# The attention gate as seven-product groups, and weight sums by DMA, in a two-layer hybrid block on one Trainium2 core

## The chip, the cores and the metric

The kernel runs on one core of one Trainium2 chip. The metric is the device time of one execution in microseconds, as the median of several runs. Beside the timed runs there is one profiled execution, from which all rows of the trace come.

## What is computed

Two layers of a block on 512 tokens and 16 meta tokens, 1024 wide, in float32. Cut to what matters here:

```
h = rms_norm(x, norm_g)
q, k, v, gate_a, u_b, gate_b, q_idx, k_idx, w_idx, merge = split(h @ w_in)
...
attn = indexer_sparse_attention(q, k, v, q_idx, k_idx, w_idx, k_top)   # top 128 keys a query
y_a = (attn * silu(gate_a)) @ w_a          # gate_a is 512 columns of w_in
y_b = (multiscale_pool(u_b) * silu(gate_b)) @ w_b
g_a, g_b = split(sigmoid(merge))           # merge is 2048 columns of w_in
return x + (g_a * y_a + g_b * y_b) @ w_out
```

## The kernel before

Every weight matrix is cut into chunks of 1 MB (256 columns of `w_in`), which are loaded, prepared and used in the order of the list `chunks`. A product in float32 is made of three matmuls of a faster type: the weights and the activations are each split into a high part (a rounded copy) and a low part (the rest), and high x high, high x low and low x high are summed in PSUM. `hhi` and `hlo` are the two parts of the normalised input.

A chunk is prepared in one of three ways. By `high`, `second` and `low` ScalarE casts and VectorE subtracts. For chunks in `by_dma`, ScalarE writes the negative low part's start, GpSimd adds the raw weights by an accumulating DMA (`minus`, L200 to L203), and ScalarE makes the high part (`plus`). The chunks in `mixed` are those of the merge gates: `mixed_prep` makes seven combinations of the chunk's four blocks a11, a12, a21, a22 (Winograd's form of a 2 x 2 block product), each as a high and a low part, in nine items `i0` to `i8`; its four sums of blocks are VectorE instructions (`mix`). The raw weights live in a ring of four half chunks (tag `raw`), so that a chunk's load waits for the chunk two ahead of it to be done with.

TensorE's order is written out by hand and so is VectorE's; ScalarE, GpSimd and the DMA queue of SyncE are ordered by a scheduler. A dense chunk (`dense`) takes 8 x 3 matmuls for each 128 output columns and each part of the tokens: two parts of 272 and 256 tokens in layer 0, one of 512 in layer 1. In `mix_gates` a chunk is a group of seven products of 12 matmuls each, 264 (layer 0) or 256 (layer 1) columns wide, whose operands are sums of the normalised input's quarters (`sums_of_h`, some by way of HBM in `far` and `hsheet`). After each product `end()` calls `group_done`, which runs what `later` has put off to this count, lets one preparation item run (and more until the list is `LEAD` ahead), and advances attention by `rate / 2` steps. `NEEDS` says which item a product waits for.

Attention is a generator (`attention`, three steps for each of 16 units u, made of two heads of one tile of 128 queries) that is woven between products by `fill` and `pump`. Its input is the top-k selection, 16 rounds of MAX8 and MATCH_REPLACE8 on VectorE, woven in by `sel` wherever the metered cost of VectorE (`dve_cost`, `FULL`) falls behind that of TensorE; `ensure` runs what is missing of it before a tile's logits. The gated result is written over `sa`, which holds the gate.

The order of a layer's stages is: keys and values with the indexer's queries; the pooled branch's gate (`sb`); the pooled branch's input; `queries(0)`; the attention gate (`sa`, two dense chunks, L1199 to L1209); `queries(1)`; the products with `w_b`, with attention woven in from here (L1224); eight seven-product groups for the merge gates; `w_a`; `w_out`.

Of the kernel before, what the change touches and what calls it, by code (L numbers as in the profile page):

```python
# [29 lines left out]
PB = 4  # L30
R_ATT = (1.95, 1.7)
FULL = 1.0
CAP = 1.5
# [47 lines left out]
def dve_cost(name, out, a=None, *rest):  # L81
    if name == "memset":
        return 0.1
    n = max(cols(out), cols(a))
    return 0.15 + n * (0.00052 if name in ("tensor_copy", "tensor_scalar") else 0.00104)


@with_exitstack
def tile_block(ctx: ExitStack, tc: tile.TileContext, x, meta, w_in, pool_w, w_a, w_b, w_out, rows, hgain, c_tab, out):
# [23 lines left out]
    mixed, by_dma, plain = set(), set(), set()  # L113
    metas = {7: 0, 10: 1}
    for l in range(2):
        wi = w_rows(w_in[l], 0, w_in.shape[2])

        chunks.append([(wi[:, :, 2176:2432], 0)])
        plain.add(len(chunks))
        chunks.append([(wi[:, :, 512:640], 0), (wi[:, :, 2688:2816], 128)])  # L120
        mb = [3784, 4040, 4296, 4552]
        order = [2432, 1664, 1920, 1408, 1152, 0, 640, 896, 256]
        chunks += [[(wi[:, :, c:c + 256], 0)] for c in order]
        chunks += [[(w_rows(w_b[l], c, 512), 0)] for c in (0, 512)]
        by_dma |= set(range(len(chunks) - 10, len(chunks)))
        mixed |= set(range(len(chunks), len(chunks) + 8))
        chunks += [[(wi[:, :, c:c + 256], 0)] for c in (*mb, 2760, 3016, 3272, 3528)]
        chunks += [[(w_rows(w_a[l], c, 512), 0)] for c in (0, 512)]
        chunks += [[(w_rows(w_out[l], c, 256), 0)] for c in (0, 256, 512, 768)]
# [4 lines left out]
    def w_place():  # L134
        c = W["load"]
        W["load"] += 1
        kt = chunks[c][0][0].shape[1]
        raws[c] = [wpool.tile([128, kt // 2, 2048 // kt], F32, tag="raw", name="raw", bufs=4) for s in range(2)]
# [25 lines left out]
    def w_prep_enqueue(casts_first=False, after=None):  # L164
# [40 lines left out]
        def plus(s):  # L205
            t = split(0)
            act.copy(t, raws[c][s])  # L207
            if s == 1:
                del raws[c]
                w_load()  # L210

        def highs():
# [11 lines left out]
        else:  # L224
            prep_q.extend((lambda: high(0), second, lambda: low(1)))

    def mixed_prep(c):

        r0, r1 = raws[c]
        blk = {"a11": r0[:, :, 0:128], "a21": r0[:, :, 128:256], "a12": r1[:, :, 0:128], "a22": r1[:, :, 128:256]}  # L230
        src = {"a11": "a11", "a12": "a12", "a22": "a22", "s3": "a11", "s2": "s2", "s1": "a21", "s4": "a12"}
        ops = ready[c]

        def hi(n):
            t = w_tile().rearrange("p (s k e) -> p s k e", s=2, k=4)
            ops[n] = t
            act.copy(t[:, 0], blk[src[n]])  # L237

        def lo(n):
            dve.tensor_sub(ops[n][:, 1], blk[src[n]], f(ops[n][:, 0]))  # L240

        def mix(eng, to, x, y, op):
            eng.tensor_tensor(blk[to], blk[x], blk[y], op=op)
# [371 lines left out]
    def q_post(t, ps, normed, dst, g=0):  # L615
# [18 lines left out]
        if normed and t == 0:  # L634
            norms()
        gp.tensor_tensor(t1[:m, :256], t1[:m, :256], t2[:m, :256], op=OP.add)
        if normed:
# [77 lines left out]
    def attention(ensure):  # L715
# [91 lines left out]

        for u in range(-1, 17):
            if u + 1 < 16:
                logits(u + 1)  # L810
# [56 lines left out]
    def sums_of_h(l, s0, n2):  # L867
# [7 lines left out]
        def sums(g):  # L875
            k = slice(2 * g, 2 * g + 2)
            a0, a1, b0, b1 = nf[0][:, k, c0], nf[0][:, k, c1], nf[1][:, k, c0], nf[1][:, k, c1]
            dve.tensor_tensor(a0, a1, a0, op=OP.subtract)
            dve.tensor_tensor(a1, b1, a1, op=OP.subtract)
            dve.tensor_tensor(b1, b1, a0, op=OP.subtract)  # L880
            dma(far[:, 0, g], a0)
# [3 lines left out]
        def lows(g):  # L885
            k = slice(2 * g, 2 * g + 2)
            a1, b0, b1 = nf[0][:, k, c1], nf[1][:, k, c0], nf[1][:, k, c1]
            dve.tensor_tensor(b0, b0, b1, op=OP.subtract)
            dma(far[:, 1, g], b0)
# [49 lines left out]
    def mix_gates(zb, ta, s0, n2, operands, splits, alos):  # L939
        base = popped[0] - progress[W["use"]]  # L940
        for q in range(8):
            c = W["use"]
# [3 lines left out]
            bs = [bank("d") for _ in range(3)]  # L946
            U, S, X = (bs[r] for r in ROLES[q % 3])
            done = [0]
# [10 lines left out]
            def end():  # L959
                done[0] += 1  # L960
                group_done()
                while prep_q and (popped[0] < base + 9 * q + LEAD + done[0] * 9 // 7 or (q == 7 and done[0] > 4)):
                    prep_one()

            def gate(eh, t, src, in_sheet):
                j = 2 * q + eh
                cs = slice(s0 + t * n2, s0 + (t + 1) * n2)
                if q < 4:
                    th = src if in_sheet else sheet(n2, "th")[:, :n2]
                    act.activation(th, src, AF.Tanh, scale=0.5)  # L970
                    d = zb[:, j, cs]
                    later(lambda: dve.scalar_tensor_tensor(d, th, 1.0, d, op0=OP.add, op1=OP.mult), 2)
                else:
                    act.activation(ta[j - KT][:, cs], src, AF.Tanh, scale=0.5)

            def total(eh, t, ps, part):
                o = sheet(n2, "c")[:, :n2]
                dve.tensor_tensor(o, ps[:, :n2], part, op=OP.add)
# [84 lines left out]
    for l in range(2):  # L1063
# [131 lines left out]

        queries(0)
        sa = one.tile([128, 4, T], F32, tag="D", name="sila")
        SIL["a"] = sa
        for c in range(2):  # L1199
            w = chunk()  # L1200
            for mi in range(2):
                j = 2 * c + mi
                for hf, a, n, o in halves:
                    ps = dense(w, mi, a, n)
                    th = sheet(n, "th")
                    act.activation(th[:, :n], ps[:, :n], AF.Tanh, scale=0.5)
                    later(lambda th=th, ps=ps, j=j, a=a, n=n: dve.scalar_tensor_tensor(
                        sa[:, j, a:a + n], th[:, :n], 1.0, ps[:, :n], op0=OP.add, op1=OP.mult), 1)
                    group_done()  # L1209
        queries(1)  # L1210

# [11 lines left out]

        fill.append(attend())  # L1224
        rate[0] = R_ATT[l]
        for _ in range(2):
# [30 lines left out]

        mix_gates(zb, ta, s0, n2, operands, splits, alos)
        drain()
# [153 lines left out]
```

## Time and profile before

| | |
|---|---|
| median of 3 runs | 758.84 us (757.47 to 760.31) |
| profiled execution | 756.37 us |
| its span, first to last instruction | 754.6 us |
| instructions in the profile | 15640 |
| granted TensorE clock | 1.00 |

PE is TensorE's matmuls, PEld its weight loads, DVE VectorE, ACT ScalarE, POOL GpSimd, SP SyncE, which issues most DMAs. Most TensorE and VectorE instructions are recorded under line 61, that of a helper, so they are told apart by their tiles: `d<-hhi,w` is a matmul of a weight tile `w` with `hhi` into the PSUM tile `d`. `lt` are attention's logits, `sc` the indexer's scores, `pm` the weights of the meta tokens, `pt` the turned weights. A matmul's own duration includes its way through the array, so the pace of TensorE is read from the distance between starts. Idle time stands in brackets, with what ended it.

### The profile page before, as it was taken

Reading aid. Unit: us, or ns where it says so; the run is one execution under the profiler, and the core shown is the slowest. Engines: PE = TensorE matmul, PEld = TensorE weight load, DVE = VectorE, ACT = ScalarE, POOL = GpSimd, SP = SyncE. Lnnn points to the kernel's source line nnn. Section 1 sums busy time; section 2 is a strip of 40 time slices with the busy share of each in tenths; the row PEclk is TensorE's granted clock in tenths of the full one; section 3 lists DMA queues with packets and bytes.
Section 4 is the critical chain, followed back from the end, with each engine's and each line's share of the span. In section 5 each row is a group of like instructions: output and inputs, shape, how many; then the busy total and the mean of one; then the engine's idle time right before and its main releaser. Section 6 shows DMA issues by size and latency. Waiting matters only on the chain.

```text
span 754.6 us, 15640 instructions
## 1 busy us (share of the span) xinstructions
PE 739.7 (98%) x5914; PEld 707.6 (94%) x5914; DVE 563.7 (75%) x1416; ACT 471.8 (63%) x1049; POOL 213.8 (28%) x280
## 2 busy tenths in 40 slices
PE   8999999999989999999999999999999999999998
PEld 7999999999989999999999989988989899999998
DVE  6866987889798775894358668787998888678531
ACT  7679645558869795543245786555677788764320
POOL 3741075242012100063256401741501011005100
PEclk9999999999999999999999999999999999999999
DMA  7677757775122223543422787667812322146411
GB/s 263 226 167 173 166 127 179 158 200 139 31 82 57 57 57 96 184 143 127 128 87 83 171 190 186 157 151 203 208 38 61 98 67 56 57 135 204 140 43 43
DMA packets 73547, 96.94 MB, mean 128 GB/s; under 512 B 3664, under 2 KB 58736, under 8 KB 73472
## 3 DMA queue, kind: packets, MB, share of 16 engines
q1 hardware_dynamic: 67632, 74.89, 31.9%
q0 software_dynamic: 5760, 20.97, 14.8%
q8 instruction: 46, 0.75, 0.4%
q14 instruction: 29, 0.24, 0.1%
q10 hardware_dynamic: 80, 0.08, 0.0%
HBM read 66.41 MB, written 8.55 MB: 99 GB/s over the span
## 4 chain that ended last, share of the span: by engine, by line
PE 81%; DVE 9%; ACT 6%; issue 1%; POOL 1%; DMA 1%; SPq 0%; DVEq 0%; ACTq 0%
PE d L61 69%; PE a L61 10%; PE v L61 3%; DVE w L61 3%; ACT lt L749 2%; ACT w L237 1%; ACT lt L760 1%; DVE raw L61 1%; DVE lt L61 1%; ACT pt L776 1%; DVE c L61 1%; DVE s L61 1%; DVE sc L61 1%; DVE alo L61 1%; DMA xt<-in_x_dram 1%
## 5 line engine op out<-in xcount | busy, mean ns | idle before, releaser
L61 PE MATMUL d<-hhi,w 128*128 128x256 f32 (+3 forms) x1408 | 287.6, 296 | 0.3 <-DVE c L61 0.2
L61 PEld LDWEIGHTS d<-hhi,w 128*128 128x128 f32 x1408 | 225.9, 188 | 6.0 <-DVE c L61 0.7
L61 PE MATMUL d<-hlo,w 128*128 128x256 f32 (+3 forms) x704 | 193.5, 294 | 0.0
L61 PEld LDWEIGHTS d<-hlo,w 128*128 128x128 f32 x704 | 132.5, 188 | 2.6 <-issue 0.2
L61 PE MATMUL d<-w,hhi 128*128 128x256 f32 x768 | 121.0, 287 | 0.5 <-DVE w L61 0.5
L61 DVE TENSOR_TENSOR w<-raw,w 128x512 fp32r<-128x512 f32 (+1 forms) x128 | 107.7, 851 | 2.4 <-ACT w L237 2.3
L61 PEld LDWEIGHTS d<-w,hhi 128*128 128x128 f32 x768 | 104.3, 188 | 5.0 <-issue 2.1
L761 POOL TENSOR_SCALAR pm<-lt,rs 128x16 f32<-128x16 f32 x48 | 27.8, 592 | 173.3 <-DVE rs L61 166.4
L61 PE MATMUL d<-hsum,w 128*128 128x264 f32 (+1 forms) x576 | 76.6, 286 | 0.0
L61 PEld LDWEIGHTS d<-hsum,w 128*128 128x128 f32 x576 | 71.7, 188 | 0.7 <-ACT lt L760 0.3
L61 PE MATMUL d<-w,hlo 128*128 128x256 f32 x384 | 72.3, 281 | 0.0
L203 POOL DMA_DIRECT2D w<-raw x40 | 36.6, 929 | 104.4 <-ACT w L202 82.6
L237 ACT CAST w<-raw 128x512 fp32r<-128x512 f32 x96 | 56.9, 624 | 2.1 <-DVE raw L61 2.0
L61 PEld LDWEIGHTS d<-w,hlo 128*128 128x128 f32 x384 | 57.0, 188 | 0.0
L1274 POOL TENSOR_TENSOR hlo<-ta,hhi 128x256 fp32r<-128x256 f32 (+1 forms) x28 | 28.2, 1019 | 96.5 <-PE d L61 83.2
L61 DVE MATCH_REPLACE8 sc<-m,sc 128x400 f32<-128x400 f32 (+2 forms) x100 | 54.3, 548 | 0.0
L61 DVE MAX8 m<-sc 128x8 f32<-128x400 f32 (+2 forms) x100 | 52.7, 556 | 0.8
L749 ACT ACTIVATE lt<-lt,mn,NR 128x144 f32<-128x144 f32 (+3 forms) x64 | 42.4, 666 | 13.9 <-DVE mn L61 13.9
L61 PE MATMUL d<-mhi,w 128*128 128x272 f32 (+2 forms) x192 | 47.7, 328 | 0.0
L202 ACT ACTIVATE w<-raw 128x1024 fp32r<-128x1024 f32 x40 | 41.4, 1057 | 8.3 <-PE d L61 8.3
L61 DVE SCALAR_TENSOR_TENSOR sc<-r,wsg,sc 128x144 f32<-128x144 f32 (+3 forms) x56 | 32.3, 580 | 16.2 <-ACT r L673 14.1
L207 ACT CAST w<-raw 128x1024 fp32r<-128x1024 f32 x40 | 41.5, 1050 | 0.0
(209 smaller groups left out, 1391.2 us busy)
## 6 DMA issues: line engine op xcount, KB each, us to landing
raw<-in_w_in_dram SPq DMA_DIRECT2D x72, 512.0 KB, 4.1
w<-raw POOLq DMA_DIRECT2D x40, 512.0 KB, 5.3
raw<-in_w_out_dram SPq DMA_DIRECT2D x16, 512.0 KB, 3.4
kept<-res SPq DMA_DIRECT2D x16, 264.0 KB, 4.0
res<-kept SPq DMA_DIRECT2D x16, 264.0 KB, 5.8
raw<-in_w_branch_b_dram SPq DMA_DIRECT2D x8, 512.0 KB, 3.8
raw<-in_w_branch_a_dram SPq DMA_DIRECT2D x8, 512.0 KB, 3.7
xt<-in_x_dram SPq DMA_DIRECT2D x4, 512.0 KB, 5.6
```

The lines of the kernel that those rows point to most:

```text
L61: return fn(*a, **k)
L202: act.activation(t, raws[c][s], AF.Copy, scale=-1.0)
L203: gp.dma_start(t, raws[c][s], accum_op=OP.add)
L207: act.copy(t, raws[c][s])
L237: act.copy(t[:, 0], blk[src[n]])
L749: act.activation(L[hh][:, :n], L[hh][:, :n], AF.Exp, scale=NR[:, i, h:h + 1], bias=mn[:, hh:hh + 1], accum_out=sm[:, hh:hh + 1])
L760: act.activation(L[hh][:, 16:n], L[hh][:, 16:n], AF.Copy, scale=rs[:, hh:hh + 1])
L761: (gp if j < 3 else dve).tensor_scalar(pms[i][:, 2 * j + hh, :], L[hh][:, 0:16], rs[:, hh:hh + 1], None, op0=OP.mult)
L776: act.copy(pt[:, :2 * len(bs)], tp[:, :256 * len(bs)].rearrange("p (a c) -> p a c", c=128))
L1274: pool_end = gp.tensor_sub(hlo[:, j, a:a + n], d, f(hhi[:, j, a:a + n]))
```

## The change

The attention gate's two chunks leave their place between `queries(0)` and `queries(1)` and become groups q = -2 and q = -1 of `mix_gates`, ahead of the eight merge groups; they are `mixed` chunks now, loaded in that order. Attention starts after the `w_b` products, at a lower rate, and its unit u = 4 waits until the gate is ready. Mixed chunks are loaded block by block, so that each block is a contiguous tile, in four DMAs instead of two. Of the sums of blocks, one (a21 + a11) is an accumulating DMA issued in item `i6` of the chunk ahead (`first_sum`; for the first mixed chunk after the last `w_b` chunk's `plus`), one (a12 + s2, for the late operand `s4`) an accumulating DMA issued in `i1`, and two stay on VectorE. For this some combinations change their sign: `sums_of_h` and the tanh of the second half follow. The planner's constants change too.

```
-R_ATT = (1.95, 1.7)
-FULL = 1.0
+R_ATT = (1.75, 1.6)
+FULL = 1.05
...
     if name == "memset":
-        return 0.1
+        return 0.08
     n = max(cols(out), cols(a))
-    return 0.15 + n * (0.00052 if name in ("tensor_copy", "tensor_scalar") else 0.00104)
+    each = 0.00052 if name in ("tensor_copy", "tensor_scalar") else 0.00104
+    return {"match_replace": 0.13, "tensor_tensor_reduce": 0.18}.get(name, 0.07) + n * each
...
-        order = [2432, 1664, 1920, 1408, 1152, 0, 640, 896, 256]
+        order = [2432, 1664, 1920, 1408, 1152, 0, 256]
...
-        chunks += [[(wi[:, :, c:c + 256], 0)] for c in (*mb, 2760, 3016, 3272, 3528)]
+        chunks += [[(wi[:, :, c:c + 256], 0)] for c in (640, 896, *mb, 2760, 3016, 3272, 3528)]
...
+        if c in mixed:
+            src = chunks[c][0][0]
+            for eh in range(2):
+                nc.sync.dma_start(raws[c][s][:, eh], src[:, 4 * s:4 * s + 4, eh * 128:eh * 128 + 128])
+            return
...
                 w_load()
+                with tc.issue_after(added[0]):
+                    first_sum(c + 1)
...
+    def first_sum(c):
+        if c in mixed:
+            gp.dma_start(raws[c][0][:, 1], raws[c][0][:, 0], accum_op=OP.add)
...
         def i0():
-            hi("a11")
+            hi("a12")
         def i1():
-            lo("a11")
-            mix(dve, "a11", "a11", "a21", OP.subtract)
-            hi("a12")
-        def i2():
             lo("a12")
             blk["s2"] = ...
-            mix(dve, "s2", "a22", "a11", OP.subtract)
-            mix(dve, "a21", "a21", "a22", OP.add)
+            dve.tensor_add(blk["s2"], blk["a21"], blk["a22"])
+            gp.dma_start(blk["a12"], blk["s2"], accum_op=OP.add)
+            hi("a11")
+        def i2():
+            lo("a11")
+            dve.tensor_sub(blk["a11"], blk["s2"], blk["a11"])
...
             lo("s2")
-            mix(dve, "a12", "a12", "s2", OP.subtract)
             hi("s1")
...
             hi("s4")
+            first_sum(c + 1)
...
         for u in range(-1, 17):
+            while u == 4 and not SIL["ready"]:
+                yield
...
-                t = tmp.tile([128, T], F32, tag="B", name="hsheet", bufs=8) if w == 0 else sheet(T, "hsheet")
+                t = sheet(T, "hsheet")
...
-    NEEDS = {"a11": 1, "a12": 2, "s2": 4, "s1": 5, "s3": 6, "s4": 7, "a22": 8}
+    NEEDS = {"a11": 2, "a12": 2, "s2": 4, "s1": 5, "s3": 6, "s4": 7, "a22": 8}
...
-        for q in range(8):
+        for q in range(-2, 8):
...
-                if q < 4:
+                if q < 0:
+                    th = sheet(n2, "th")[:, :n2]
+                    act.activation(th, src, AF.Tanh, scale=0.5)
+                    d = sa[:, j + 4, cs]
+                    later(lambda: dve.scalar_tensor_tensor(d, th, sign, src, op0=OP.add, op1=OP.mult),
+                          3 if in_sheet else 2)
+                elif q < 4:
...
             product(S, "s4", False)
+            total(0, 1, S, u)
             end()
             product(U, "a22", False)
-            total(0, 1, S, u)
             gate(1, 0, U[:, :n2], False)
...
+            if q == -1:
+                later(lambda: SIL.update(ready=True), 4)
...
         queries(0)
+        queries(1)
         sa = one.tile([128, 4, T], F32, tag="D", name="sila")
-        SIL["a"] = sa
-        for c in range(2):
-            w = chunk()
...
-        queries(1)
+        SIL.update(a=sa, ready=False)
...
-        fill.append(attend())
-        rate[0] = R_ATT[l]
...
         last_sum()
+        fill.append(attend())
+        rate[0] = R_ATT[l]
```

More of the change, by code (lines that the diff above doesn't have):

```diff
@@ L113, in tile_block @@
     mixed, by_dma, plain = set(), set(), set()
-    metas = {7: 0, 10: 1}
+    metas = {7: 0, 8: 1}
     for l in range(2):
@@ L121, in tile_block @@
         mb = [3784, 4040, 4296, 4552]
-        order = [2432, 1664, 1920, 1408, 1152, 0, 640, 896, 256]
+        order = [2432, 1664, 1920, 1408, 1152, 0, 256]
         chunks += [[(wi[:, :, c:c + 256], 0)] for c in order]
         chunks += [[(w_rows(w_b[l], c, 512), 0)] for c in (0, 512)]
-        by_dma |= set(range(len(chunks) - 10, len(chunks)))
-        mixed |= set(range(len(chunks), len(chunks) + 8))
-        chunks += [[(wi[:, :, c:c + 256], 0)] for c in (*mb, 2760, 3016, 3272, 3528)]
+        by_dma |= set(range(len(chunks) - 8, len(chunks)))
+        mixed |= set(range(len(chunks), len(chunks) + 10))
+        chunks += [[(wi[:, :, c:c + 256], 0)] for c in (640, 896, *mb, 2760, 3016, 3272, 3528)]
         chunks += [[(w_rows(w_a[l], c, 512), 0)] for c in (0, 512)]
@@ L137, in w_place @@
         kt = chunks[c][0][0].shape[1]
-        raws[c] = [wpool.tile([128, kt // 2, 2048 // kt], F32, tag="raw", name="raw", bufs=4) for s in range(2)]
+        shape = [128, 2, 4, 128] if c in mixed else [128, kt // 2, 2048 // kt]
+        raws[c] = [wpool.tile(shape, F32, tag="raw", name="raw", bufs=4) for s in range(2)]
         return c
@@ L225, in w_prep_enqueue @@
             prep_q.extend((lambda: high(0), second, lambda: low(1)))
+    added = [None]
+    def first_sum(c):
+        if c in mixed:
+            gp.dma_start(raws[c][0][:, 1], raws[c][0][:, 0], accum_op=OP.add)
     def mixed_prep(c):
         r0, r1 = raws[c]
-        blk = {"a11": r0[:, :, 0:128], "a21": r0[:, :, 128:256], "a12": r1[:, :, 0:128], "a22": r1[:, :, 128:256]}
-        src = {"a11": "a11", "a12": "a12", "a22": "a22", "s3": "a11", "s2": "s2", "s1": "a21", "s4": "a12"}
+        blk = {"a11": r0[:, 0], "a21": r0[:, 1], "a12": r1[:, 0], "a22": r1[:, 1]}
+        src = {"a11": "a11", "a12": "a12", "a22": "a22", "s3": "a21", "s2": "s2", "s1": "a11", "s4": "a12"}
         ops = ready[c]
@@ L635, in q_post @@
             norms()
-        gp.tensor_tensor(t1[:m, :256], t1[:m, :256], t2[:m, :256], op=OP.add)
+        added[0] = gp.tensor_tensor(t1[:m, :256], t1[:m, :256], t2[:m, :256], op=OP.add).ins
         if normed:
@@ L877, in sums @@
             a0, a1, b0, b1 = nf[0][:, k, c0], nf[0][:, k, c1], nf[1][:, k, c0], nf[1][:, k, c1]
-            dve.tensor_tensor(a0, a1, a0, op=OP.subtract)
+            dve.tensor_tensor(a0, a0, a1, op=OP.subtract)
             dve.tensor_tensor(a1, b1, a1, op=OP.subtract)
-            dve.tensor_tensor(b1, b1, a0, op=OP.subtract)
+            dve.scalar_tensor_tensor(b1, b1, -1.0, a0, op0=OP.mult, op1=OP.subtract)
             dma(far[:, 0, g], a0)
@@ L887, in lows @@
             a1, b0, b1 = nf[0][:, k, c1], nf[1][:, k, c0], nf[1][:, k, c1]
-            dve.tensor_tensor(b0, b0, b1, op=OP.subtract)
+            dve.scalar_tensor_tensor(b0, b1, -1.0, b0, op0=OP.mult, op1=OP.subtract)
             dma(far[:, 1, g], b0)
@@ L946, in mix_gates @@
             bs = [bank("d") for _ in range(3)]
-            U, S, X = (bs[r] for r in ROLES[q % 3])
+            U, S, X = (bs[r] for r in ROLES[(q + 2) % 3])
             done = [0]
@@ L961, in end @@
                 group_done()
-                while prep_q and (popped[0] < base + 9 * q + LEAD + done[0] * 9 // 7 or (q == 7 and done[0] > 4)):
+                while prep_q and (popped[0] < base + 9 * (q + 2) + LEAD + done[0] * 9 // 7 or (q == 7 and done[0] > 4)):
                     prep_one()
@@ L966, in gate @@
                 j = 2 * q + eh
+                sign = -1.0 if eh else 1.0
                 cs = slice(s0 + t * n2, s0 + (t + 1) * n2)
-                if q < 4:
+                if q < 0:
[5 more added lines that the diff above has]
+                elif q < 4:
                     th = src if in_sheet else sheet(n2, "th")[:, :n2]
-                    act.activation(th, src, AF.Tanh, scale=0.5)
+                    act.activation(th, src, AF.Tanh, scale=0.5 * sign)
                     d = zb[:, j, cs]
@@ L973, in gate @@
                 else:
-                    act.activation(ta[j - KT][:, cs], src, AF.Tanh, scale=0.5)
+                    act.activation(ta[j - KT][:, cs], src, AF.Tanh, scale=0.5 * sign)
             def total(eh, t, ps, part):
-                o = sheet(n2, "c")[:, :n2]
+                cs = slice(s0 + t * n2, s0 + (t + 1) * n2)
+                o = sa[:, 2 * q + eh + 4, cs] if q < 0 else sheet(n2, "c")[:, :n2]
                 dve.tensor_tensor(o, ps[:, :n2], part, op=OP.add)
@@ L1196, in tile_block @@
         queries(0)
+        queries(1)
         sa = one.tile([128, 4, T], F32, tag="D", name="sila")
-        SIL["a"] = sa
-        for c in range(2):
-            w = chunk()
[L1201 to L1209, printed above, removed]
-        queries(1)
+        SIL.update(a=sa, ready=False)
         def attend():
@@ L1256, in alos @@
                 dve.tensor_sub(alo[:, :, a:a + n], sa[:, :, a:a + n], f(ahi[:, :, a:a + n]))
-        mix_gates(zb, ta, s0, n2, operands, splits, alos)
+        mix_gates(sa, zb, ta, s0, n2, operands, splits, alos)
         drain()
```

4 lines of the change are left out of this document (1 added, 3 removed).

## The prediction

> **What bounds the kernel now.** I read the page's busy line and its chain first, then the busy times of the stages that the change touches, then TensorE's order of work inside them.
>
> ```profile
> span 754.6 us, 15640 instructions
> PE 739.7 (98%) x5914; PEld 707.6 (94%) x5914; DVE 563.7 (75%) x1416; ACT 471.8 (63%) x1049; POOL 213.8 (28%) x280
> PEclk9999999999999999999999999999999999999999
> ...
> PE 81%; DVE 9%; ACT 6%; issue 1%; POOL 1%; DMA 1%; SPq 0%; DVEq 0%; ACTq 0%
> ```
> ```profile
> 128.80:154.00 25.20, 25.20 (x212) 24.90 (x210) 22.04 (x59) 15.45 (x28) 8.86 (x10) 1.00 0.57 126
> 167.45:201.70 34.25, 34.25 (x295) 33.78 (x294) 30.88 (x96) 28.72 (x80) 7.81 (x14) 1.00 0.35 90
> ...
> 201.70:315.20 113.50, 109.66 (x954) 106.11 (x952) 90.66 (x231) 85.50 (x200) 10.38 (x16) 1.00 0.27 78
> ...
> 566.00:679.50 113.50, 111.09 (x985) 107.10 (x985) 90.72 (x233) 88.83 (x208) 12.57 (x18) 1.00 0.27 80
> ```
>
> The second fence has a row a stage: its bounds and length, then busy time of PE, PEld, DVE, ACT and POOL, granted clock, DMA share, GB/s. TensorE is the bound, at full clock. The rows are layer 0's attention gate (128.80), layer 0's `w_b` products (167.45) and the seven-product stages of both layers (201.70, 566.00). TensorE never idles in the first two. In the seven-product stages it idles 113.50 - 109.66 = 3.8 us and 113.50 - 111.09 = 2.4 us, while VectorE and ScalarE are busy 75 to 80%. So time goes if TensorE issues less work, or if those 6.2 us shrink; it comes back if VectorE, ScalarE or a late sum makes TensorE wait.
>
> **1. The gate's arithmetic: -5.0 us.** A chunk of 256 gate columns takes 96 matmuls now (48 of 512 columns in layer 1) and 84 as seven products. The rows are start, length, engine, tiles, count.
>
> ```profile
> 90.36 1.28 PE L61 MATMUL d<-hhi,w 128*128 128x272 f32 x9
> 102.02 1.29 PE L61 MATMUL d<-hhi,w 128*128 128x272 f32 x9
> 297.16 4.66 PE L61 MATMUL d<-hsum,w 128*128 128x264 f32 x36
> 307.48 4.55 PE L61 MATMUL d<-hsum,w 128*128 128x264 f32 x36
> 512.71 2.25 PE L61 MATMUL d<-hhi,w 128*128 128x512 f32 x9
> 518.28 2.25 PE L61 MATMUL d<-hhi,w 128*128 128x512 f32 x9
> ```
> ```profile
> 678.08 24.23 PE d L61 x204
> ```
>
> Layer 0: from 90.36 to 102.02 two blocks of both token halves are issued, which is a chunk: 11.66 us. From 297.16 to 307.48 lies one group of seven without attention in it: 10.32 us. Gain 1.34 a chunk, 2.7 for two. Layer 1: 518.28 - 512.71 = 5.57 us for 24 wide matmuls (232 ns each), so 11.14 a chunk; the chain's row gives 24.23/204 = 118.8 ns for 256 columns, so 84 take 9.98. Gain 1.16, 2.3 for two. Together 5.0 us.
>
> A rule speaks against this step. The Trainium skill, "TensorE: Matmul & The Clock Gate", section "Back-to-back issue gap", gives a sustained 81 ns for 128 columns and 131 ns for 512 where every matmul has its own weight load; interpolated, as an estimate, halving the width would cost layer 1 about 3.8 us instead of gaining 2.3, and the step would come to +1.5 us in all. This trace's 232 ns for 512 columns contradicts it, so I leave it 1 chance in 100, inside the flat rival.
>
> **2. The weights' preparation: off the path, more room per group.**
>
> ```profile
> L61 DVE TENSOR_TENSOR w<-raw,w 128x512 fp32r<-128x512 f32 x96 | 64.8, 683 | 2.4 <-ACT w L237 2.3
> L61 DVE TENSOR_TENSOR raw<-raw 128x512 f32<-128x512 f32 x32 | 22.0, 687 | 0.6
> L237 ACT CAST w<-raw 128x512 fp32r<-128x512 f32 x96 | 56.9, 624 | 2.1 <-DVE raw L61 2.0
> L61 DVE TENSOR_TENSOR c<-d,p 128x264 f32<-128x264 f32 x16 | 6.8, 428 | 10.3 <-PE d L61 6.9 <-ACT lt L749 1.8 <-ACT lt L760 1.5
> ...
> L983 ACT COPY p<-d 128x264 f32<-128x264 f32 x16 | 6.0, 375 | 1.7 <-PE d L61 1.7
> L61 DVE SCALAR_TENSOR_TENSOR zb<-c,zb 128x264 f32<-128x264 f32 x12 | 5.1, 427 | 5.2 <-ACT c L970 5.2
> ...
> L970 ACT ACTIVATE c<-c 128x264 f32<-128x264 f32 x12 | 5.0, 421 | 0.5 <-DVE c L61 0.5
> ```
>
> A mixed chunk has seven lows and four sums on VectorE, 11 x 0.685 = 7.5 us; two sums go to DMA, leaving 6.2. The 16 old chunks save 16 x 2 x 0.685 = 21.9 us; each new group brings 6.2 + 3 totals of 0.428 + 4 gates of 0.427 = 9.2, or 36.8 for four. ScalarE pays per new group 7 x 0.624 + 3 x 0.375 + 4 x 0.421 = 7.2 us. For layer 0's `w_b` and seven-product stages together, VectorE goes from 121.5 to 121.5 - 11.0 + 18.4 = 129 us and ScalarE from 114.2 to 128.6, while TensorE's time there goes from 147.8 to about 167 (two groups of 10.32, less the waits): 82% becomes 77% on VectorE, ScalarE stays at 77%. Neither becomes the bound. The four chunks' old preparation, four ScalarE passes and two GpSimd transfers each, goes from stages in which TensorE waited for nothing. The changed signs swap one pass for another on the same tiles: nothing. One sheet moves to the ring of six that attention uses, at a time when attention no longer runs: nothing.
>
> **3. Loads and sums by DMA: 0 us, bounds 0 and +18.**
>
> ```profile
> raw<-in_w_in_dram SPq DMA_DIRECT2D x72, 512.0 KB, 4.1
> w<-raw POOLq DMA_DIRECT2D x40, 512.0 KB, 5.3
> ...
> raw<-in_w_in_dram SPq DMA_DIRECT2D x8, 256.0 KB, 4.6
> ```
> ```profile
> L203 POOL DMA_DIRECT2D w<-raw x40: 849/874/1218, 43.6 to 540.0; - x40
> ...
> DMA to landing us min/median/max: 4.4/5.3/9.4
> ```
>
> A chunk comes in four loads of 256 KB with 512-byte rows instead of two of 512 KB; the eight such loads in the trace land after 4.6 us, and DMA is busy 27% of the stage. Nothing of a sum inside a buffer is in the trace; nearest are GpSimd's 40 accumulating transfers of twice the size: issue 0.87 us, landing 4.4 to 9.4, median 5.3. I take 5.3 as the safe side for half the bytes. The first sum is issued in item 6 of the chunk ahead and read in item 1, four items later; a group with attention takes about 14.4 us for nine items, so 6.4 us. TensorE's next product asks for an item two behind those already issued, 3.2 us more. So a sum must take over 9.6 us from its issue before TensorE waits. The sum for `s4` has five items, 8 us. On GpSimd's queue the sums stand among the `pm` scalings; a scaling is read only once in four steps of attention, so a sum ahead of it costs nothing unless it waits for its load, issued seven items (11 us) earlier.
>
> **4. Attention moves behind `w_b`: -1.9 us.**
>
> ```profile
> 217.41 1.18 DVE L61 MAX8 m<-sc 128x8 f32<-128x400 f32 x2
> 219.72 0.70 DVE L61 TENSOR_SCALAR sc<-sc 128x400 f32<-128x400 f32 x2
> 220.61 0.91 ACT L760 ACTIVATE lt<-lt,rs 128x256 f32<-128x256 f32 x2 [2.31 <-DVE rs L61]
> 221.17 0.95 PE L61 MATMUL a<-consts,lt 128*128 128x128 f32 x4 [1.90 <-ACT lt L760]
> ```
>
> Now attention takes 16 of its 60 steps beside `w_b`, and its second tile pair meets a top-k that is not finished: VectorE is made to finish it, the scaling waits 2.31 us for a reciprocal behind it, and TensorE idles 1.90 us. In the changed order the last top-k round of layer 0 stands near the start of the seven-product stage, well ahead of that pair's logits, so this wait goes. Next late there are the small waits for exponentials and scalings; they come per attention step, whose number is unchanged, so I keep the other 4.3 us as they are. The 0.875 and 0.8 steps a product (1.75/2, 1.6/2) give 61 and 56 steps in 70 products, against 60 and 54 wanted and a short wait for the gate at step 15. `w_b` without attention is TensorE alone. The gates read one bank two products longer; its next user comes three products later, 1.5 us of cover.
>
> **5. The tail: +1.0 us, bounds 0 and 2.**
>
> ```profile
> 313.65 0.39 PE L61 MATMUL d<-hhi,w 128*128 128x264 f32 x1 [0.17 <-DVE c L61]
> ...
> 315.40 0.39 ACT L974 ACTIVATE ta<-d 128x264 f32<-128x264 f32 x1 [0.40 <-PE d L61]
> ```
>
> In the changed order attention ends about three products before the stage does (ten in layer 0 before, where TensorE lost 0.17 us). Layer 0's last cast of the attention output then stands behind the last tanh, which starts 0.40 us after the products and takes 0.39; the first `w_a` matmul needs that cast. I take 0.8 us in layer 0 and 0.2 in layer 1, where the first block doesn't read the last tile.
>
> **Sum.** -5.0 + 0 - 1.9 + 1.0 = -5.9 us. The profiled execution took 756.37 us (1.8 outside its span) and becomes 750.5; the median of the runs, 758.84, lies 2.5 above it, so by that yardstick 752.9, which I give.
>
> **The rivals.**
>
> *Late sums (slower).* If a sum takes 10.6 us rather than 5.3, each of the 18 first sums issued inside the stages makes VectorE, and behind it TensorE, wait 1 us: 752.9 + 18 = 771; at half that lateness past the point, 762. It decides from 9.6 us on. For it: one transfer took 9.4, and VectorE is in order, so the totals that free TensorE's banks queue behind a late sum. Against it: half the bytes, a quiet stage. The Trainium skill, "SBUF — State Buffer", section "SBUF: two separate sides", says that GpSimd's descriptors wait while VectorE holds the shared port in a two-port pass; no run here shows it.
>
> *Gain given back (flat).* TensorE is quicker but waits as much more in longer stretches of casts and tanh: the 5.0 us go, 757.9. For it: the longest remaining waits there follow ScalarE. Against it: VectorE's share falls and ScalarE's stays.
>
> **How the numbers follow.** Forecast 0.68 (746 to 757.5, its upper end with a two-us tail and a third of the waits more), flat rival 0.16, late sums 0.16. A half per cent, 3.8 us, is about what a measurement of this kernel can tell from no change; the line is 755.0. Of the forecast 0.62 lies below it and 0.06 above; with the flat rival that is 0.22 within, and 0.16 slower. The range, 746 to 764, takes in the flat case and the milder half of the late sums.
>
> **What would show it.** Right: 168 more narrow matmuls of 264 and of 256 in place of the wide ones; no MAX8 burst ahead of a TensorE wait; landings of the 40 new sums under 6 us; TensorE's idle time about 4 us over both seven-product stages, and under 1 at each tail. Wrong: VectorE's `s` waiting for a DMA, TensorE's waits growing with the groups, or seven-product groups over 10.4 us without attention.

## The result and the profile after

The changed kernel takes 754.32 us, the median of five runs (754.25 to 755.05), against 758.84 us for five runs of the kernel before: a ratio of 0.9942, with a 95% interval of 0.9924 to 0.9961. The forecast was 752.9 with a range of 746 to 764. The size is nearly right; most of the reasons are not.

In some executions, of any of these kernels, TensorE was granted half its clock for 3 to 4 us near the start, which costs about 1.7 us (below, first experiment); the run then has a mean clock of 0.997 or 0.998, as all five of the changed kernel have, instead of 0.999 or 1.000. Stage by stage I therefore compare the *body*: from the first matmul `a<-us,pw`, which comes after that stretch, to the end of the span, in each kernel's profiled execution. Before, it is 754.6 - 105.86 = 648.7 us; after, 753.3 - 108.01 = 645.3. A body is one execution: the profiled one of the changed kernel is the longest of its five (755.05 us), 0.7 us above their median, so differences of a microsecond between bodies say little. Where a microsecond or two matters, I set runs of equal clock side by side.

The page of the changed kernel, the lines that answer to those of before: span, busy times, shares of the chain, and three groups of DMAs.

```profile
span 753.3 us, 15956 instructions
PE 736.4 (98%) x5962; PEld 709.1 (94%) x5962; DVE 568.5 (75%) x1436; ACT 476.7 (63%) x1077; POOL 236.3 (31%) x312
...
PE 82%; DVE 13%; ACT 2%; DMA 1%; issue 1%; POOL 1%; SPq 0%; DVEq 0%; ACTq 0%
...
raw<-in_w_in_dram SPq DMA_DIRECT2D x88, 256.0 KB, 3.2
...
raw<-raw POOLq DMA_DIRECT2D x20, 256.0 KB, 4.4
raw<-s POOLq DMA_DIRECT2D x20, 256.0 KB, 3.2
```

VectorE's share of the chain went up, from 9% to 13%, where the prediction had it under less load. The stages show where. A row is the bounds and the length, then busy time of PE, PEld, DVE, ACT and POOL, granted clock, DMA share, GB/s. In turn: the start; layer 0's `w_b` products and its seven-product stage; the first 30 us of that stage in two rows, and a stretch later in it; the same of layer 1.

```profile
0.00:24.00 24.00, 21.39 (x136) 19.29 (x136) 14.97 (x42) 15.23 (x38) 8.99 (x19) 0.93 0.82 274
146.49:171.84 25.35, 25.21 (x209) 24.88 (x209) 25.25 (x64) 15.04 (x35) 8.79 (x10) 1.00 0.67 155
171.84:314.08 142.24, 138.57 (x1207) 135.19 (x1205) 112.80 (x308) 112.01 (x274) 26.13 (x41) 1.00 0.47 112
171.84:185.00 13.16, 11.56 (x96) 11.35 (x95) 12.90 (x35) 8.00 (x22) 2.02 (x4) 1.00 0.32 85
185.00:200.00 15.00, 14.53 (x121) 14.27 (x120) 14.83 (x45) 12.94 (x38) 4.37 (x7) 1.00 0.61 133
260.00:290.00 30.00, 30.00 (x276) 29.15 (x274) 20.47 (x60) 24.20 (x56) 6.10 (x10) 1.00 0.46 107
513.86:537.10 23.24, 23.24 (x110) 18.86 (x109) 23.14 (x60) 13.10 (x24) 7.33 (x9) 1.00 0.68 151
537.10:677.52 140.42, 136.26 (x1199) 132.44 (x1197) 108.84 (x300) 110.65 (x269) 26.35 (x41) 1.00 0.47 111
```

Over its whole seven-product stage VectorE is busy 112.80 of 142.24 us, 79%, which looks harmless. But it is busy 25.25 of 25.35 us beside `w_b`, 12.90 of 13.16 and 14.83 of 15.00 in the two rows behind it, and 20.47 of 30.00 later on. It is saturated for 53 us and has a third of its time free afterwards. TensorE idles 142.24 - 138.57 = 3.7 us in the stage, 1.6 of them in the first 13 us, and 140.42 - 136.26 = 4.2 us in layer 1: 7.8 us together, where before it was 6.2.

The timeline of the entry shows one such wait; the number in brackets is TensorE's idle time and what ended it.

```profile
173.59 0.69 DVE L61 MATCH_REPLACE8 sc<-m,sc 128x528 f32<-128x528 f32 x1
...
174.20 1.18 DVE L61 MAX8 m<-sc 128x8 f32<-128x400 f32 x2
...
175.30 1.37 DVE L61 TENSOR_TENSOR hsum<-hsheet,hsum 128x528 fp32r<-128x528 f32 x3
...
176.59 0.68 DVE L61 TENSOR_TENSOR w<-s,w 128x512 fp32r<-128x512 f32 x1
...
177.33 1.35 PE L61 MATMUL d<-hsum,w 128*128 128x264 f32 x9 [1.60 <-DVE w L61]
```

VectorE goes without a gap from a top-k round (MATCH_REPLACE8, MAX8) to the sums of the normalised input to a low part of the weights (`w<-s,w`, done at 177.27), and TensorE waits 1.60 us for that last one. The same wait in layer 1, at 542.56, is 1.40 us.

### The profile page after: what moved, and what is told of

It is laid out like the page before. It is cut to its first block, busy times and chain, and to the rows that moved or that the text cites. A ratio compares the mean times of both kernels' runs of the same rounds, so it can differ in the third digit from the quotient of the medians.

```text
span 753.3 us, 15956 instructions
## 1 busy us (share of the span) xinstructions
PE 736.4 (98%) x5962; PEld 709.1 (94%) x5962; DVE 568.5 (75%) x1436; ACT 476.7 (63%) x1077; POOL 236.3 (31%) x312
## 4 chain that ended last, share of the span: by engine, by line
PE 82%; DVE 13%; ACT 2%; DMA 1%; issue 1%; POOL 1%; SPq 0%; DVEq 0%; ACTq 0%
PE d L61 67%; PE a L61 11%; PE v L61 4%; DVE w L61 2%; DVE sc L61 2%; DVE m L61 2%; DVE t L61 1%; ACT w L252 1%; DVE qs L61 1%; DMA xt<-in_x_dram 1%; DMA raw<-s 1%; DVE nf L61 0%; DVE ss L61 0%; ACT lt L761 0%; DVE s L61 0%
## 5 line engine op out<-in xcount | busy, mean ns | idle before, releaser
L61 PE MATMUL d<-hhi,w 128*128 128x256 f32 (+3 forms) x1344 | 268.6, 291 | 1.3 <-DVE w L61 1.0
L61 PEld LDWEIGHTS d<-hhi,w 128*128 128x128 f32 x1344 | 214.3, 188 | 4.9 <-DVE w L61 1.7
L61 PE MATMUL d<-hlo,w 128*128 128x256 f32 (+3 forms) x672 | 182.9, 289 | 0.0
L61 DVE TENSOR_TENSOR w<-raw,w 128x512 fp32r<-128x512 f32 (+1 forms) x152 | 124.1, 825 | 5.2 <-ACT w L252 5.1
L61 PE MATMUL d<-hsum,w 128*128 128x264 f32 (+1 forms) x720 | 96.6, 286 | 3.0 <-DVE w L61 3.0
L61 PEld LDWEIGHTS d<-hsum,w 128*128 128x128 f32 x720 | 89.9, 188 | 3.9 <-DVE w L61 3.4
L252 ACT CAST w<-raw 128x512 fp32r<-128x512 f32 x120 | 70.5, 622 | 7.4 <-DVE raw L61 5.3
L210 POOL DMA_DIRECT2D w<-raw x32 | 29.6, 943 | 72.4 <-ACT w L209 51.4
L240 POOL DMA_DIRECT2D raw<-raw x20 | 18.1, 906 | 95.2 <-DMA raw<-in_w_in_dram 59.6
L265 POOL DMA_DIRECT2D raw<-s x20 | 18.4, 922 | 73.5 <-DVE c L61 21.1
```

Of the source, the lines that this page charges most:

```text
L61: return fn(*a, **k)
L210: gp.dma_start(t, raws[c][s], accum_op=OP.add)
L240: gp.dma_start(raws[c][0][:, 1], raws[c][0][:, 0], accum_op=OP.add)
L265: gp.dma_start(blk["a12"], blk["s2"], accum_op=OP.add)
```

## The experiments

Medians; each ratio is to the kernel before, run on the same chip.

| kernel | us | ratio (95%) | body, us |
|---|---|---|---|
| b_again (before, once more) | 758.13 | 1.0001 (0.9990 to 1.0012) | 648.7 |
| e_plan | 775.66 | 1.0243 (1.0222 to 1.0264) | 668.4 |
| e_sumdve | 765.82 | 1.0111 (1.0093 to 1.0130) | 657.1 |
| e_dense | 754.60 | 0.9957 (0.9942 to 0.9972) | 644.8 |
| e_bar2 | 754.19 | 0.9949 (0.9931 to 0.9966) | 645.6 |
| e_dplan | 750.94 | 0.9912 (0.9894 to 0.9930) | 642.8 |
| e_first | 757.31 | 0.9986 (0.9973 to 0.9999) | 647.5 |
| e_late | 761.29 | 1.0049 (1.0033 to 1.0066) | 654.7 |
| e_after8 | 747.80 | 0.9876 (0.9854 to 0.9897) | 639.0 |
| e_dplan8 | 753.24 | 0.9942 (0.9925 to 0.9959) | 643.3 |
| e_dplan_w0 | 752.19 | 0.9925 (0.9909 to 0.9942) | 643.2 |
| e_rate | 754.92 | 0.9953 (0.9938 to 0.9968) | 644.9 |

**b_again: the kernel before, unchanged.** The changed kernel's five runs all had a granted clock of 0.997 or 0.998. Is that the change's doing, or a matter of the single run?

> The kernel before, unchanged, to see the granted clock of each of its runs. In the profiled execution of the changed kernel TensorE runs at half clock from 10.8 to 14.3 us (mean clock 0.998), in that of the kernel before it does not (1.000). If this stretch is a matter of the single run and not of the change, runs of the kernel before fall into two groups: about 757 us at clock 1.000 and about 759 us at 0.998, 1.7 us apart. If it belongs to the changed kernel alone, all runs here show 1.000, and the spread of 757 to 760 has another source. Ratio to the kernel before 1.00 in either case.

Of its twelve runs those with a mean clock of 0.999 or 1.000 lie near 756.8 us and those with 0.997 or 0.998 near 758.5. The profile of one of the latter shows the stretch:

```profile
10.60:17.96 7.36, 7.36 (x36) 7.12 (x40) 7.36 (x19) 5.68 (x15) 2.08 (x3) 0.77 0.83 308
```

So the stretch is a matter of the single run, also of the kernel before; it is worth 1.7 us, and the body, 648.7 us twice, is free of it.

**e_plan: the changed kernel with the old constants of the planner.**

```
-FULL = 1.05
+FULL = 1.0
 # and dve_cost as it was: 0.1 for a memset, 0.15 us + n * (0.00052 or 0.00104)
```

> The changed kernel with the planner's old constants for VectorE (FULL 1.0, a fixed cost of 0.15 for each instruction): fewer top-k rounds are woven into the stages ahead. Theory: the changed kernel waits 1.60 and 1.40 us at the entry of the seven-product stages because top-k rounds stand ahead of a weight's low part in VectorE's order; the old constants thin them out there, both waits shrink below 0.5 us, and unless a later burst brings them back the time falls by 2 us, to about 752. Rival (the entry waits for the sum by DMA, not for top-k): both waits stay at 1.4 to 1.6 us and the time at 754. Second rival (the new constants are what keeps the burst away that cost 1.9 us before): the wait comes back at the second tile pair and the time rises by 2 us, to 756.

The time rose by 21 us, where the second rival had 2. With the old constants the top-k is not finished when the second tile pair's logits ask for it, and VectorE is made to finish it in one burst. Two rows of waits (total, times, longest, us), the first matmul after the longest one, and the windows around it:

```profile
PE d L61 <- DVE w L61: 16.3, 6, 14.7
PE a L61 <- ACT lt L771: 9.4, 1, 9.4
```
```profile
239.91 1.47 PE L61 MATMUL d<-hsum,w 128*128 128x264 f32 x5 [14.69 <-DVE w L61]
```
```profile
225.00:240.00 15.00, 0.31 (x3) 0.10 (x2) 14.96 (x43) 2.54 (x6) 0.00 (x0) 0.66 0.00 1
240.00:255.00 15.00, 15.00 (x123) 14.69 (x124) 10.68 (x29) 9.06 (x23) 2.44 (x5) 0.89 0.48 106
```

VectorE is busy 14.96 of 15.00 us while TensorE does almost nothing. The entry's waits of 1.60 and 1.40 us, on the other hand, are gone. So top-k work stands either in front of the entry's weights or in front of the later logits, and with attention behind `w_b` the constants that bring it forward are worth 21 us (775.66 against 754.32).

**e_sumdve: the changed kernel with all four sums on VectorE.**

```
             # item i1
+            dve.tensor_add(blk["a21"], blk["a21"], blk["a11"])
             dve.tensor_add(blk["s2"], blk["a21"], blk["a22"])
-            gp.dma_start(blk["a12"], blk["s2"], accum_op=OP.add)
             # item i4
+            dve.tensor_add(blk["a12"], blk["a12"], blk["s2"])
             # after the last w_b chunk, and item i6
-            first_sum(c + 1)
```

> The changed kernel with all four sums of weight blocks on VectorE, none by DMA: 40 more VectorE instructions of 0.685 us, 27 us in all, two a group. Theory that the gain comes from the gate's arithmetic and VectorE has room: within 2 us of the changed kernel, 753 to 756. Rival (the two sums moved to DMA are what pays, because VectorE is nearly the bound of the seven-product stages): 6 us or more slower than the changed kernel, 760 or more, with TensorE's waits for w, c and s grown in every group. Rival (late sums by DMA cost more than they save): faster by 1 to 2 us, and the wait of 0.98 us after a sum of 4.13 us in layer 0 is gone.

11.5 us are lost for 40 instructions of 0.69 us (by the medians; the body, 657.1 us, holds a second half-clock stretch, at 400 us). TensorE's waits for weights, and the first 68 us of the stage:

```profile
PE d L61 <- DVE w L61: 10.9, 15, 1.3
```
```profile
171.71:200.00 28.29, 25.15 (x201) 24.06 (x200) 27.19 (x76) 19.89 (x58) 2.28 (x6) 1.00 0.29 76
200.00:240.00 40.00, 38.19 (x332) 37.08 (x330) 37.49 (x103) 31.80 (x80) 3.70 (x8) 1.00 0.27 70
```

VectorE is now full for 40 us longer, and TensorE idles 28.29 - 25.15 = 3.1 and 40.00 - 38.19 = 1.8 us in these two rows.

**e_dense: the sums and loads by DMA alone.** The gate stays dense in its old place, attention starts at the `w_b` products, and the planner's constants and rates are those of before.

```
-R_ATT = (1.75, 1.6)
-FULL = 1.05
+R_ATT = (1.95, 1.7)
+FULL = 1.0
-        order = [2432, 1664, 1920, 1408, 1152, 0, 256]
+        order = [2432, 1664, 1920, 1408, 1152, 0, 640, 896, 256]
...
-        for q in range(-2, 8):
+        for q in range(8):
...
         queries(0)
+        # the dense gate loop of before
         queries(1)
+        fill.append(attend())      # ahead of the w_b products, not behind
```

> The changed sums and loads alone: the attention gate stays two dense chunks between the queries, attention starts beside the w_b products, with the planner's old constants. Theory (the gate's arithmetic is the gain): 757 to 760, as the kernel before, less at most 1 us. Rival (the sums by DMA are the gain): about 754, as the changed kernel.

The part that the prediction put at nothing brings 3.9 us in the body (648.7 to 644.8), about as much as the whole change (3.4 us). It is the loads in four parts and both sums together; no run has the loads alone.

**e_bar2: the changed kernel without top-k at the entry.** From the last half of the last `w_b` chunk to the end of the first group, no round is woven in.

```
-        while spare[0] > 0 and sel:
+        while spare[0] > 0 and sel and not barred[0]:
...
+                barred[0] = c == 1 and mi > 1     # w_b products
...
+            barred[0] = False                     # after a group
```

> The changed kernel with no top-k rounds woven in from the second half of the last w_b chunk to the end of the first seven-product group; they are taken up after it, and all still stand ahead of the second tile pair's logits. Theory (the entry waits of 1.60 and 1.40 us come from top-k rounds ahead of a weight's low part on VectorE): both fall below 0.4 us and the time by 2 to 3 us, to 751 to 752. Rival (VectorE has no room anywhere in these stages, so the rounds only move): the waits at the entry go and as much appears in the groups after it, time 754 to 755. Second rival (the low part itself is late because of the sum by DMA): the waits stay, time 754.

The entry is clean now, and the next 15 us are not. Windows, then the waits there:

```profile
171.77:185.00 13.23, 13.23 (x113) 13.23 (x111) 10.08 (x30) 9.61 (x26) 2.43 (x4) 1.00 0.50 115
185.00:200.00 15.00, 12.73 (x101) 12.07 (x100) 14.90 (x44) 11.09 (x34) 3.77 (x6) 1.00 0.48 111
```
```profile
192.27 0.39 PE L61 MATMUL d<-hhi,w 128*128 128x264 f32 x1 [0.46 <-ACT p L1006]
...
194.83 0.39 PE L61 MATMUL d<-hhi,w 128*128 128x264 f32 x1 [0.85 <-DVE sila L61]
...
197.97 0.51 PE L61 MATMUL d<-hhi,w 128*128 128x264 f32 x2 [0.96 <-DVE w L61]
```

The body is 645.6 us against 645.3. The wait has moved by 20 us and is no smaller (15.00 - 12.73 = 2.3 us): it is not the order of VectorE's work at the entry that costs the time, but how much of it there is before attention needs the top-k.

**e_dplan: e_dense with the new constants.**

```
-FULL = 1.0
+FULL = 1.05
 # and dve_cost as in the changed kernel
```

> Sums and loads by DMA, dense gate in its old place, attention from the w_b products on, but with the planner's new constants (the run with the old ones gave 754.6). Theory (the new constants belong to the gate's move and only keep top-k from piling up): within 1.5 us of 754.6. Rival (they bring top-k forward for a gain of their own, which the changed kernel then owes to them): 752 or less.

750.94 us, the lowest yet, though four of its six runs have no half-clock stretch. Its rows are the two seven-product stages (layer 0, layer 1) and the first 14 us of layer 0's:

```profile
196.12:312.68 116.56, 115.17 (x1009) 111.86 (x1008) 82.68 (x215) 90.41 (x210) 19.11 (x29) 1.00 0.45 108
560.47:674.08 113.61, 112.62 (x1009) 110.00 (x1007) 82.02 (x216) 90.43 (x213) 20.08 (x31) 1.00 0.46 109
196.10:210.00 13.90, 13.90 (x124) 13.59 (x123) 10.36 (x28) 11.10 (x30) 2.27 (x4) 1.00 0.41 95
```

TensorE idles 1.4 and 1.0 us in them, 2.4 in all, against 7.8 in the changed kernel, and VectorE is busy 10.36 of 13.90 us at the entry. The body is 2.0 us shorter than e_dense's and 2.5 us shorter than the changed kernel's. The runs of equal clock (0.998) say less: 752.52 and 753.84 us here, 754.25 to 755.05 for the changed kernel, on another chip. So leaving the gate and attention where they were is better by 1 to 2.5 us.

**e_first and e_late: one of the two sums back on VectorE.** In e_first the sum for the late operand returns (item `i4`), in e_late the one made a chunk ahead (item `i1`).

```
 # e_first
-            gp.dma_start(blk["a12"], blk["s2"], accum_op=OP.add)     # i1
+            dve.tensor_add(blk["a12"], blk["a12"], blk["s2"])        # i4
 # e_late
+            dve.tensor_add(blk["a21"], blk["a21"], blk["a11"])       # i1
-            first_sum(c + 1)                                         # both places
```

> The changed kernel with the late sum (a12 + s2) back on VectorE and the first sum (a21 + a11) by DMA: 20 VectorE instructions of 0.69 us more, one a group. All four sums on VectorE gave 765.8 against 754.3. Theory (VectorE is the bound of the seven-product stages, each instruction more costs nearly its length): about half way, 759 to 761. Rival (the first sum's place ahead of everything is what counts): 754 to 756. Second rival (the late sum by DMA costs as much as it saves, as its landing of 4.13 us behind a GpSimd scaling ended in a wait of 0.98 us): 753 or less.

> The changed kernel with the first sum (a21 + a11) back on VectorE and the late sum (a12 + s2) by DMA, also 20 VectorE instructions more. Theory (only the number of VectorE instructions counts): the same as with the late sum on VectorE, 759 to 761. Rival (the first sum's place counts, since s2, s1 and s3 hang on it): 762 or more here and 756 or less there.

Against the changed kernel's 754.3, e_first lost 3.0 us and e_late some 8: at a clock of 0.998 they take 757.4 us (median of five runs) and 762.3 and 762.8 (two runs). (Medians of all runs would set e_late too low, since five of its eight have no half-clock stretch; its body holds a second stretch, at 639 us.) Together that is the 11.5 us of e_sumdve. It is the same 20 instructions of 0.69 us in both, so VectorE's load alone does not explain the difference. The sum made ahead is also the one that stands first in a chunk's preparation, with everything of `s2` behind it; the other has four items of room. That its place in the chain of a chunk makes the remaining 5 us is my reading; no run isolates it.

**e_after8 and e_dplan8: half the top-k.** Both kernels with 8 of the 16 rounds, so that VectorE has some 48 us less to do; the selection is then of 64 keys.

```
-        for rnd in range(16):
+        for rnd in range(8):
```

> The changed kernel with the top-k selection cut to its first 8 of 16 rounds (the rest of the selection is left out), some 27 us less VectorE work a layer. To be set against the next run, which has the same cut with the dense gate. Theory (the gate's 5.0 us of TensorE are returned because VectorE is full in the first 30 us of the stage, 97 to 99% busy, with top-k on top of the weights' preparation): with the cut the waits there go and this kernel is 4 to 5 us faster than the next one. Rival (the seven products cost TensorE itself more than reckoned, or the waits come from ScalarE's or attention's order): it stays 2 to 4 us slower than the next one, as without the cut (754.3 against 750.9).

> Sums and loads by DMA and the new constants, dense gate in its old place, attention from the w_b products on, with the top-k selection cut to 8 of 16 rounds (the rest is left out). TensorE idles only 2.4 us in its two seven-product stages with all 16 rounds, so the cut brings at most 3 us: 748 to 751, under either theory; the difference from the run above decides.

The changed kernel drops by 6.3 us in the body (645.3 to 639.0), the one with the dense gate not at all (642.8 to 643.3). With VectorE relieved the seven-product gate is ahead by 4.3 us in the body, and by about 4 in runs of equal clock (748.93 us against 752.58 to 753.30 at 0.998); the prediction's step 1 says 5.0. The medians, 5.4 apart, set four runs of six with the half-clock stretch against one of five. The changed kernel's entry, relieved:

```profile
174.12:187.10 12.98, 12.98 (x111) 12.98 (x109) 9.85 (x29) 9.04 (x26) 2.42 (x4) 1.00 0.48 113
```

TensorE waits for nothing there any more.

**e_dplan_w0: e_dplan with a longer warm-up,** 24 matmuls ahead of the first work instead of 16, against the half clock at the start.

```
-W0 = 16
+W0 = 24
```

> Sums and loads by DMA and the new constants, dense gate in its old place, attention from the w_b products on (750.9), with 24 idle matmuls at the start instead of 16. Theory of the start (the half-clock stretch of 3.4 us at about 11 us follows when TensorE stands idle between the idle matmuls and the first transposes): all runs at clock 0.999 or 1.000, none near 752.5; the median stays at 750.8 or loses what the longer warm-up delays, at most 1 us. Rival (the stretch has another cause): runs at 0.998 remain, 1.7 us slower.

752.19 us: no gain. Four of its five runs had a clock of 1.000, one of 0.998, so the stretch is not gone for sure, and the longer warm-up takes time at the start: the first `a<-us,pw` comes at 107.0 us instead of 106.2 (e_dplan, both profiled at clock 1.000). The medians, 752.19 against 750.94, are from two chips. What sets off the stretch stays open.

**e_rate: the changed kernel with attention's rate raised,** so that it ends earlier in the stage.

```
-R_ATT = (1.75, 1.6)
+R_ATT = (1.95, 1.8)
```

> The changed kernel with attention at 0.975 and 0.9 steps a product (R_ATT 1.95 and 1.8) instead of 0.875 and 0.8, so that it ends some seven products earlier. Theory (the waits at the tail, 0.61 us in layer 0 and about as much in layer 1's w_a, come from attention's end close to the stage's): those 1.2 us go, but the same VectorE work falls in a shorter stretch, and its first groups are already full: 754 to 757. Rival (the low rate is what makes the stage wait): 752 or less.

The tail's waits go (the `w_a` stage of layer 1 takes 21.96 us instead of 22.61), and three of 0.69, 1.19 and 0.80 us come inside the stage, while the entry's 1.63 and 1.40 stay: 754.92 us, no gain.

## Why the forecast was nearly right, point by point

In the body, from kernel to kernel, the change of -3.4 us is made of: the sums and loads by DMA -3.9 (before to e_dense), the planner's constants -2.0 (e_dense to e_dplan), the gate as seven products with attention behind `w_b` +2.5 (e_dplan to the changed kernel). The forecast of -5.9 had them at 0, at 0 and at -5.9. Each difference is of two profiled executions; in runs of equal clock the three steps are -3.8, -2.1 and +1.1, the last two across chips and the last from two runs of e_dplan. The shares hold for this order of the steps only: taken out of the changed kernel by themselves, the constants are worth 21 us and the sums 11.5. No run separates the gate's move from attention's.

**Step 1 (gate's arithmetic, -5.0): right as work of TensorE, not as time.** e_after8 against e_dplan8 shows most of it, 4.3 us. The bodies of e_dplan and the changed kernel, then of e_dplan8 and e_after8 (length, TensorE's busy time):

```profile
106.20:749.00 642.80, 635.64 (x5110) 608.40 (x5108) 462.44 (x1170) 398.43 (x880) 192.45 (x250) 1.00 0.52 131
108.01:753.30 645.29, 632.00 (x5158) 607.82 (x5156) 486.63 (x1222) 402.45 (x908) 193.22 (x250) 1.00 0.50 128
```
```profile
110.09:753.40 643.31, 636.11 (x5110) 608.85 (x5108) 413.79 (x1028) 398.19 (x880) 192.03 (x250) 1.00 0.51 131
110.65:749.70 639.05, 630.22 (x5158) 607.17 (x5156) 438.06 (x1082) 401.01 (x908) 194.78 (x250) 1.00 0.51 129
```

With the seven products TensorE is busy 3.6 us less in the first pair and 5.9 in the second, but its idle time rises from 7.2 to 13.3 us in the first and only from 7.2 to 8.8 in the second. In the changed kernel the gain came back as waits, which is step 2's doing.

**Step 2 (preparation, "neither becomes the bound"): failed.** It forecast 129 us of VectorE and 128.6 of ScalarE over layer 0's `w_b` and seven-product stages, in about 167 us. Measured: 25.25 + 112.80 = 138.1 of VectorE and 15.04 + 112.01 = 127.1 of ScalarE in 167.6. Length and ScalarE are right, VectorE is 9 us short, and its share did not fall to 77% but stayed at 82%. What was left out is the top-k. In those two stages it took, before and then after (groups of VectorE: count, then busy us and mean ns):

```profile
L61 DVE MATCH_REPLACE8 sc<-m,sc 128x528 f32<-128x528 f32 (+1 forms) x15 | 9.3, 629 | 0.0
L61 DVE MAX8 m<-sc 128x8 f32<-128x400 f32 (+1 forms) x14 | 8.2, 628 | 0.0
```
```profile
L61 DVE MATCH_REPLACE8 sc<-m,sc 128x400 f32<-128x400 f32 (+1 forms) x24 | 14.8, 625 | 0.0
...
L61 DVE MAX8 m<-sc 128x8 f32<-128x400 f32 (+1 forms) x22 | 13.0, 630 | 0.0
```

17.5 us became 27.8. The dense gate had stood ahead of `w_b`, and in its 25.20 us the kernel before ran 14.5 us of those rounds while TensorE waited for nothing:

```profile
L61 DVE MATCH_REPLACE8 sc<-m,sc 128x400 f32<-128x400 f32 (+1 forms) x12 | 7.4, 625 | 0.0
L61 DVE MAX8 m<-sc 128x8 f32<-128x400 f32 (+1 forms) x12 | 7.1, 630 | 0.0
```

With the gate moved, rounds that had room there meet the mixed chunks' preparation. And a share averaged over 167 us could not show it: the load stands in the first 53 us. The Trainium skill says in "Perfetto Trace Analysis", section "Optimization Strategy", that a kernel can have several regimes with a different most-contended engine in each. Here they lie inside one stage: VectorE 98 to 99% busy in its first 28 us, 68% in the row of 260 to 290 us.

**Step 3 (loads and sums by DMA, 0): the cost was right, the worth was left out.** The sums' own cost is near nothing: they land after 4.4 and 3.2 us in the median, 6.7 and 5.1 at most, nearly the "under 6" asked for. Their worth was put at nothing as well, because VectorE was taken as hidden: a saving of 21.9 us there was entered in step 2 and given no price. It is worth 3.9 us where the gate stays dense, and 11.5 us in the changed kernel.

**Step 4 (attention behind `w_b`, -1.9): half right.** The burst and its 1.90 us wait are gone, but the new constants do this: with the gate and attention moved and the old constants (e_plan), the wait is 8 times as long, and with the new constants and attention left beside `w_b` (e_dplan) no wait in layer 0's stage is over 0.6 us. "I keep the other 4.3 us as they are" failed: TensorE idles 7.8 us in the two stages, 0.61 of them the tail of step 5.

**Step 5 (tail, +1.0): right in size.** Layer 0's `w_a` waits 0.61 us for the cast of the attention output, and layer 1's `w_a` takes 0.64 us more; the prediction had 0.8 and 0.2.

**The rivals.** *Late sums* did not happen, but for one place, which the chain of waits shows (start, length, what):

```profile
196.17 0.57 POOL pm L773
196.74 4.13 DMA raw<-s
200.87 0.02 issue
200.89 0.84 ACT w L252 x2
...
203.43 0.62 PE a L61 x2
```

A sum issued behind a `pm` scaling on GpSimd's queue holds up a cast, a scaling of attention's logits (`lt`, L772) behind that, and TensorE by 0.98 us. *Gain given back* did happen, beside e_dplan by the gate's whole gain and more (6.1 us of idle time for 3.6 of work), but through VectorE, which the prediction had ruled out, and not through ScalarE. That the total came out near the forecast is luck: the sums and the constants, put at nothing, paid it back.

## What to carry to other kernels

Read an engine's load in windows as long as one step of the pipeline, not as the mean of a stage: 79% over 142 us hid 28 us at 98%, and it was those that cost the time. When work is moved, ask what the place that it leaves was hiding: here the dense gate had covered the top-k. And run each part of a combined change by itself: the part that was thought free was the gain, and the part that was thought the gain cost 1 to 2.5 us; the kernel without it took 750.94 us.

## What the runs showed of the hardware

The granted clock of TensorE halves for a stretch early in some executions (0.50 from 11 to 14 us in the changed kernel's). By the row from 0 to 24 us this stretch is (1 - 0.93) x 24 / 0.5 = 3.4 us in the changed kernel, in which TensorE was not idle: in the kernel before, run again, it was busy 7.36 of the 7.36 us around it. In e_sumdve such a stretch came at 400 us as well: a clock of 0.83 over 10.00 us, in which TensorE was busy 10.00. In e_plan the clock also halved after TensorE had begun its wait of 14.69 us: by the two rows (1 - 0.66) x 15 / 0.5 = 10.2 us and then (1 - 0.89) x 15 / 0.5 = 3.3 us after the work had resumed, which adds some 1.6 us to the wait. The Trainium skill, "TensorE: Matmul & The Clock Gate", section "HAM oscillation — how this bites in real kernels", says that idle gaps above some 3.4 us bring the clock down; e_plan agrees, with a gap of 14.69 us: the clock was 1.00 for its first 4 us and 0.50 after 5. The stretches at the start and at 400 us, with TensorE busy around them, are not explained by that rule as far as these rows show.
